# The passages between the sublayers of a hybrid encoder block: one function in a fixed engine order

## The chip, the cores and the metric

The kernel runs on one core of one Trainium2 chip. Its engines work side by side, each through its own queue in order: TensorE (PE) multiplies, VectorE (DVE), ScalarE (ACT) and GpSimd (POOL) work element by element, and SyncE (SP) issues most DMAs. The metric is the device time of one execution in microseconds; for the kernel before it is the median of three runs.

## The reference

One encoder layer over 256 tokens of width 2048, in float32, with three sublayers. A vector c gives, through one large matrix (`w_ada`), a shift, a scale and a gate for each sublayer:

```python
mod = (silu(c) @ w_ada + b_ada)          # 3 x (shift, scale, gate), 2048 each
modulate(h, s) = layer_norm(h) * (1 + scale[s]) + shift[s]

y = swiglu(modulate(x, 0), ffn1_w13, ffn1_w2)                 # d_ff = 5632
x = layer_norm(ALPHA * x + 0.5 * gate[0] * y, ln_g[0], ln_b[0])

proj = modulate(x, 1) @ w_in + b_in      # q, k, v, o, gates, x_rg, g_rg
y = concat(mLSTM(...) , RG-LRU(...)) @ w_out
x = layer_norm(ALPHA * x + gate[1] * y, ln_g[1], ln_b[1])

y = swiglu(modulate(x, 2), ffn2_w13, ffn2_w2)
x = layer_norm(ALPHA * x + 0.5 * gate[2] * y, ln_g[2], ln_b[2])
```

ALPHA is 2 to the power 1/4. Between two sublayers there is thus a chain that nothing can go around: the last products of y, the residual, the statistics of a row, the post-norm with its gain and bias, the statistics again, the second normalisation, a transpose, the modulation, and only then the first products of the next sublayer.

## The kernel before

**Precision.** Every float32 operand of a matmul is split in two float32r parts, high and low, and each product is three matmuls (high x high, high x low, low x high). `load_w` (L80) does that for a weight tile of 128 x 2048: a DMA on SP's queue into one of four raw buffers (L83), a copy to the high part on ACT (L92), a subtraction to the low part on DVE (L95). Three buffers of each kind ("hi", "lo") hold the parts; a fourth pair can come out of the six general slots (`spare`, L64). With `fine` set, both run in four pieces of 512 columns.

**Work.** x stays in SBUF as two row tiles of 128 tokens (t = 0, 1). A sublayer's input u is kept transposed as `uh` and `ul`. `stat_w` (L260) has the weights stationary and moves 256 tokens: 48 matmuls of 128 x 256 per weight tile. `mov_t` (L271) has the activations of one row tile stationary and moves 512 weight columns: 12 matmuls for each weight tile and row tile. `ffn` (L332) goes through groups of hidden columns: g1 makes a group's hidden rows, g2 (L479) multiplies the group before with w2 and adds into yacc (L494). The mixer (L549) runs projections (`proj`, L562), gates, recurrence, heads and the output product.

**adaLN tiles.** The product with w_ada is 144 tiles of 128 x 2048, each a DMA on SP and one DVE instruction with an accumulator (L136). `tick` (L144) hands them out: every weight load adds a rate to a credit, and each whole credit issues one tile. The rates stand in a table (L36 to L39); `ada_until` (L139) forces those that are needed.

**A passage before.** `tail` (L301) makes the last products of a sublayer for row tile 0 and then 1 (tiles named tl), with `residual` (L316) behind each: DVE multiplies with the gate (L320), then DVE or POOL adds to x (L322, L325), and DVE takes statistics (L327). `post_ln` (L236) normalises: DVE three quarters in six instructions (L250, L252), ACT and POOL the last (L245 to L247), then the statistics of the result (L256). `after` (L819) makes the second normalisation n (L190, L191). In the middle of row tile 1 `ahead` loads and splits the first three weight tiles of the next sublayer. `front` (L289) then takes both row tiles in turn: `modulate_t` (L210) makes all sixteen transposes (tu, L216) in four groups, modulates them on ACT and DVE (L221, L223) and splits them (L224, L225); then come the 48 matmuls of that row tile. Credits run on through all of it.

**Order.** The tile framework orders each engine's queue itself, by priorities and a simulated time; the program's text does not fix it.

**Gate columns.** Among the projections `gates` (L611) makes the mLSTM's gates on DVE, in small instructions on 4 x 256, and `gate_cols` (L622) transposes them on PE (pcol, L626 and L627). It stands behind the third pair of x_rg tiles (L687).

Of the kernel before, what the change touches and what calls it, by code (L numbers as in the profile page):

```python
# [15 lines left out]
P = 128  # L16
D = 2048
# [33 lines left out]
def block_kernel(ctx: ExitStack, tc: tile.TileContext, a: dict, out: bass.AP):  # L51
# [28 lines left out]
    def load_w(src, name, into=None):  # L80
        tick()
        raw = raw_tile("r" + name)
        nc.sync.dma_start(raw, src)  # L83
        if into is None:
            hi = wp.tile([P, 2048], F32R, tag="hi", bufs=3, name="h" + name)
            lo = wp.tile([P, 2048], F32R, tag="lo", bufs=3, name="l" + name)
        else:
            hi, lo = into()
        step = 512 if fine[0] else 2048
        for c in range(0, 2048, step):  # L90
            w = slice(c, c + step)
            nc.scalar.copy(hi[:, w], raw[:, w])  # L92
        for c in range(0, 2048, step):
            w = slice(c, c + step)
            nc.vector.tensor_sub(lo[:, w], raw[:, w], hi[:, w].bitcast(F32))  # L95
        return hi, lo

# [87 lines left out]
    def normed(st, t, n, nm, on_vector=0):  # L185

        mv, r, b = moments(st, nm)
        c = on_vector
        if c:
            nc.vector.tensor_scalar(n[:, 0:c], x[:, t, 0:c], mv[:, 0:1], r, op0=ALU.subtract, op1=ALU.mult)  # L190
        nc.scalar.activation(n[:, c:], x[:, t, c:], AF.Identity, bias=b, scale=r)  # L191
# [18 lines left out]
    def modulate_t(s, t, n):  # L210

        tk = slice(t * P, (t + 1) * P)
        for kt in range(0, KT, 4):
            ps = bank(f"tu{s}{t}_{kt}")
            for j in range(4):
                nc.tensor.transpose(ps[:, j * P:(j + 1) * P], n[:, (kt + j) * P:(kt + j + 1) * P], ident)  # L216
            u = sm.tile([P, 4, P], F32, tag="u", bufs=2, name=f"u{s}{t}_{kt}")
            for j in range(4):
                b, g = modc[:, s, 0, kt + j:kt + j + 1], modc[:, s, 1, kt + j:kt + j + 1]
                if j < MOD_ACT[t]:  # L220
                    nc.scalar.activation(u[:, j, :], ps[:, j * P:(j + 1) * P], AF.Identity, bias=b, scale=g)  # L221
                else:
                    nc.vector.tensor_scalar(u[:, j, :], ps[:, j * P:(j + 1) * P], g, b, op0=ALU.mult, op1=ALU.add)  # L223
            nc.scalar.copy(uh[:, kt:kt + 4, tk], u)  # L224
            nc.vector.tensor_sub(ul[:, kt:kt + 4, tk], u, uh[:, kt:kt + 4, tk].bitcast(F32))  # L225

# [8 lines left out]

    def post_ln(s, t, st, gb):  # L236

        nm = f"p{s}{t}"  # L240
        g, b = gb
        mv, r, nb = moments(st, nm)
        out_st = sm.tile([P, 4, 6], F32, tag="st", name="st" + nm)
        c = slice(AFF, D)
        nc.scalar.activation(x[:, t, c], x[:, t, c], AF.Identity, bias=nb, scale=r)  # L245
        nc.gpsimd.tensor_mul(x[:, t, c], x[:, t, c], g[:, c])
        nc.gpsimd.tensor_add(x[:, t, c], x[:, t, c], b[:, c])  # L247
        for k in range(0, AFF, 512):
            c = slice(k, k + 512)
            nc.vector.scalar_tensor_tensor(x[:, t, c], x[:, t, c], mv[:, 0:1], g[:, c],  # L250
                                           op0=ALU.subtract, op1=ALU.mult)
            nc.vector.scalar_tensor_tensor(x[:, t, c], x[:, t, c], r, b[:, c],  # L252
                                           op0=ALU.mult, op1=ALU.add)
        if s < 2:
            for n in range(4):
                nc.vector.bn_stats(out_st[:, n, :], x[:, t, n * 512:(n + 1) * 512])  # L256
        return out_st
# [13 lines left out]
    def mov_t(ps, hl, acth, actl, k0, t, first, last):  # L271

        hi, lo = hl
        tk = slice(t * P, (t + 1) * P)
        for j in range(4):
            w = slice(j * 512, (j + 1) * 512)
            nc.tensor.matmul(ps, acth[:, k0 + j, tk], hi[:, w], start=first and j == 0, stop=False)  # L277
            nc.tensor.matmul(ps, acth[:, k0 + j, tk], lo[:, w], start=False, stop=False)  # L278
            nc.tensor.matmul(ps, actl[:, k0 + j, tk], hi[:, w], start=False, stop=last and j == 3)  # L279
# [5 lines left out]
    def front_tiles(tiles, nm, ks):  # L285
        return [load_w(tiles[k], f"{nm}{k}", spare if k == 3 else None)
                for k in ks]

    def front(s, ns, hls, tiles, nm):  # L289

        hls = hls + front_tiles(tiles, nm, range(len(hls), 4))
        pss = [bank(f"{nm}{t}") for t in range(NT)]
        for t in range(NT):
            modulate_t(s, t, ns[t])
            if t == NT - 1:
                fine[0] = False
            for k in range(4):
                mov_t(pss[t], hls[k], uh, ul, k * 4, t, k == 0, k == 3)
        return pss

    def tail(s, blocks, mm, alpha, sts, gb, ahead):  # L301


        for t in range(NT):
            for i, n in enumerate(blocks):
# [642 lines left out]
```

## Time and profile before

| | |
|---|---|
| median of three runs | 2034.55 us (2031.8 to 2035.66) |
| the profiled execution | 2032.17 us |
| its span, first to last instruction | 2030.4 us |
| mean granted TensorE clock | 0.981 |
| HBM read | 509.22 MB, 252 GB/s over the span |

The profile is of one execution. A row of its timeline has the start in us, the duration in us, the engine, the line, the operation, output <- input, the shapes and the count, and in brackets the idle time before it with what ended it. A row of groups has a bar, then busy time and mean ns of one, and a second bar, then the idle time before them. A row of windows has for each stretch its length, the busy time of PE, PEld, DVE, ACT and POOL with counts, then the granted clock, the share of the DMA engines and GB/s. A row of waits has the waiting instruction, what released it, the sum in us, how often, and the longest. Matmuls are pipelined: a matmul of 128 x 512 is listed with 0.39 us, though the next can start after less.

### The profile page before, as it was taken

To read this page: it belongs to the slowest core of one execution; us is meant where nothing else is said; L and a number is where in the kernel's file an instruction comes from. 1 tells how busy PE (TensorE), PEld (TensorE's weight loads), DVE (VectorE), ACT (ScalarE), POOL (GpSimd) and SP (SyncE) were. 2 spreads that over 40 slices of the span, in tenths; PEclk is the share of its full clock that TensorE was granted. 3 is DMA by queue.
4 is the path that set the end of the run, shared out by engine and by line. 5 is a ranking of instruction groups with operands and counts; after the bars stand their busy time and mean duration, and the time that the engine had idled before them with its cause. 6 is when DMAs were issued, how large, how long until landed. Compare 5 with 4: busy or idle time off the path is not lost.

```text
span 2030.4 us, 30188 instructions
## 1 busy us (share of the span) xinstructions
PE 1926.2 (95%) x13068; PEld 1788.7 (88%) x13068; DVE 1435.2 (71%) x1340; ACT 814.2 (40%) x752; POOL 58.6 (3%) x76
## 2 busy tenths in 40 slices
PE   7899999999999997597999997999999999999996
PEld 6899998799899985497989885899999899899985
DVE  7998898987978889876785778544444544544558
ACT  5433344443334332643743334533443333334332
POOL 0000000000000001200000002000000000000003
PEclk8999999999999999798999998999999999999998
DMA  9998888999998997475677565455555555555552
GB/s 385 340 352 299 306 329 330 359 350 352 367 348 321 351 336 282 160 285 189 241 275 273 208 212 182 166 184 179 184 192 177 194 185 181 195 179 178 193 187 104
DMA packets 72709, 513.27 MB, mean 253 GB/s; under 512 B 8448, under 2 KB 8576, under 8 KB 10880
## 3 DMA queue, kind: packets, MB, share of 16 engines
q1 hardware_dynamic: 69984, 501.25, 67.4%
q10 hardware_dynamic: 2592, 10.09, 1.3%
q8 instruction: 102, 1.67, 0.3%
q14 instruction: 31, 0.25, 0.0%
HBM read 509.22 MB, written 2.10 MB: 252 GB/s over the span
## 4 chain that ended last, share of the span: by engine, by line
PE 87%; DVE 9%; issue 2%; DMA 1%; ACT 1%; POOL 0%; POOLq 0%; SPq 0%; DVEq 0%
PE py L278 6%; PE py L277 6%; PE py L279 6%; PE pg L269 6%; PE pv L268 6%; PE pv L267 6%; PE pv L269 6%; PE pg L268 6%; PE pg L267 6%; PE pj L267 3%; PE pj L269 3%; PE pj L268 3%; DVE ada L136 2%; PE rg L268 2%; PE rg L269 2%
## 5 line engine op out<-in xcount | busy, mean ns | idle before, releaser
L136 DVE CUSTOM_DVE_ANT_0 ada<-ada,scb,badac 128x2048 f32<-128x2048 f32 x144 | 340.0, 2364 | 11.4 <-DMA ada<-in_w_ada 9.6
L269 PE MATMUL pg<-uh,lg 128*128 128x256 f32 x960 | 272.1, 283 | 0.5 <-DVE lg L95 0.5
L269 PE MATMUL pv<-uh,lv 128*128 128x256 f32 x960 | 271.8, 283 | 0.0
L267 PE MATMUL pg<-uh,hg 128*128 128x256 f32 x960 | 271.7, 283 | 0.0
L268 PE MATMUL pv<-ul,hv 128*128 128x256 f32 x960 | 271.7, 283 | 0.0
L267 PE MATMUL pv<-uh,hv 128*128 128x256 f32 x960 | 271.7, 283 | 0.0
L268 PE MATMUL pg<-ul,hg 128*128 128x256 f32 x960 | 271.7, 283 | 0.0
L95 DVE TENSOR_TENSOR lw<-rw,hw 128x2048 fp32r<-128x2048 f32 x80 | 183.3, 2291 | 123.1 <-ACT hw L92 123.1
L278 PE MATMUL py<-lw,hth 128*128 128x512 f32 x640 | 250.3, 391 | 3.7 <-DVE lw L95 3.5
L95 DVE TENSOR_TENSOR lv<-rv,hv 128x2048 fp32r<-128x2048 f32 x68 | 155.8, 2291 | 134.5 <-ACT hv L92 134.5
L279 PE MATMUL py<-hw,htl 128*128 128x512 f32 x640 | 249.1, 389 | 0.0
L92 ACT CAST hw<-rw 128x2048 fp32r<-128x2048 f32 x80 | 152.8, 1911 | 231.0 <-DMA rw<-in_w 73.9
L277 PE MATMUL py<-hw,hth 128*128 128x512 f32 x640 | 242.7, 390 | 0.0
L95 DVE TENSOR_TENSOR lg<-rg,hg 128x2048 fp32r<-128x2048 f32 x60 | 137.5, 2292 | 114.5 <-ACT hg L92 114.5
L92 ACT CAST hv<-rv 128x2048 fp32r<-128x2048 f32 x68 | 129.6, 1906 | 210.9 <-PE pg L268 76.1
L269 PEld LDWEIGHTS pg<-uh,lg 128*128 128x128 f32 x960 | 184.3, 192 | 1.1 <-DVE lg L95 1.1
L92 ACT CAST hg<-rg 128x2048 fp32r<-128x2048 f32 x60 | 114.2, 1904 | 175.4 <-PE pv L268 108.3
L268 PEld LDWEIGHTS pg<-ul,hg 128*128 128x128 f32 x960 | 184.3, 192 | 0.3
L267 PEld LDWEIGHTS pg<-uh,hg 128*128 128x128 f32 x960 | 184.3, 192 | 0.3
L269 PEld LDWEIGHTS pv<-uh,lv 128*128 128x128 f32 x960 | 184.3, 192 | 0.0
L267 PEld LDWEIGHTS pv<-uh,hv 128*128 128x128 f32 x960 | 184.3, 192 | 0.0
L268 PEld LDWEIGHTS pv<-ul,hv 128*128 128x128 f32 x960 | 184.3, 192 | 0.0
(363 smaller groups left out, 4186.8 us busy)
## 6 DMA issues: line engine op xcount, KB each, us to landing
ada<-in_w_ada SPq DMA_DIRECT2D x144, 1024.0 KB, 5.8
rw<-in_w SPq DMA_DIRECT2D x80, 1024.0 KB, 4.8
rg<-in_w SPq DMA_DIRECT2D x60, 1024.0 KB, 4.9
rv<-in_w SPq DMA_DIRECT2D x60, 1024.0 KB, 4.8
rra<-in_w_r SPq DMA_DIRECT2D x48, 1024.0 KB, 5.2
rs<-in_w_s SPq DMA_DIRECT2D x32, 1024.0 KB, 4.8
rwo<-in_w_out SPq DMA_DIRECT2D x16, 1024.0 KB, 4.7
ro<-in_w_vo SPq DMA_DIRECT2D x8, 1024.0 KB, 4.8
```

The source lines that it names most:

```text
L92: nc.scalar.copy(hi[:, w], raw[:, w])
L95: nc.vector.tensor_sub(lo[:, w], raw[:, w], hi[:, w].bitcast(F32))
L136: nc.vector.tensor_tensor_reduce(raw, raw, scb, 1.0, badac[:, s, j, kt:kt + 1], ALU.mult, ALU.add, adac[:, s, j, kt:kt + 1])
L267: nc.tensor.matmul(ps, hi[:, w], uh[:, k0 + j, :], start=st, stop=False)
L268: nc.tensor.matmul(ps, hi[:, w], ul[:, k0 + j, :], start=False, stop=False)
L269: nc.tensor.matmul(ps, lo[:, w], uh[:, k0 + j, :], start=False, stop=sp)
L277: nc.tensor.matmul(ps, acth[:, k0 + j, tk], hi[:, w], start=first and j == 0, stop=False)
L278: nc.tensor.matmul(ps, acth[:, k0 + j, tk], lo[:, w], start=False, stop=False)
L279: nc.tensor.matmul(ps, actl[:, k0 + j, tk], hi[:, w], start=False, stop=last and j == 3)
```

## The change

One function, `boundary`, takes the place of `tail`, `front`, `modulate_t`, `post_ln` and `after`. It issues on DVE, ACT, POOL and TensorE through a wrapper that pins each instruction behind the one traced before it on its engine. The next sublayer's four weight tiles are all loaded at its start; those named in `ready` are split between the residuals of row tile 0, the others between the blocks of row tile 0, one of them with its low part on POOL. Part of the last weights go into uh and ul, whose contents are no longer needed. The credits are zero within a passage. x is scaled by ALPHA beforehand on ACT, so that a residual only adds; the earlier blocks' residuals move to POOL, and those within a passage run on DVE alone. The gate columns move from behind the third to behind the fourth pair of tiles (from 4 to 6).

```diff
-    def load_w(src, name, into=None):
+    def load(src, name, into=None):
         tick()
         raw = raw_tile("r" + name)
         nc.sync.dma_start(raw, src)
+        return raw, name, into
+    def split(tile, act, low):
+        raw, name, into = tile
+        hi, lo = into() if into else [wp.tile([P, 2048], F32R, tag=w, bufs=3, name=w[0] + name) for w in ("hi", "lo")]
         step = 512 if fine[0] else 2048
+        cols = [slice(c, c + step) for c in range(0, 2048, step)]
+        for w in cols:
+            act.copy(cut(hi, w), like(raw[:, w], hi))
+        for w in cols:
+            low.tensor_sub(cut(lo, w), like(raw[:, w], lo), cut(hi, w).bitcast(F32))
         return hi, lo
+    class Pinned:
...
+        def __getattr__(self, op):
+            def issue(*args, **kw):
+                ins = getattr(self.engine, op)(*args, **kw)
+                tc.keep_in_program_order(ins)
+                return ins
+            return issue
+    V, A, G, T = (Pinned(e) for e in (nc.vector, nc.scalar, nc.gpsimd, nc.tensor))
...
+    def half(t):
+        return lambda: [u[:, :, t * P:(t + 1) * P] for u in (uh, ul)]
+    def rows(k):
+        return lambda: [u[:, k:k + 8, :].rearrange("p a b -> p (a b)") for u in (uh, ul)]
-    def residual(s, t, n, y, alpha, sts):
+    def residual(s, t, n, y, sts):
...
-        nc.vector.tensor_mul(g, y, gate[:, c])
-        if alpha:
-            nc.vector.scalar_tensor_tensor(x[:, t, c], x[:, t, c], ALPHA, g, op0=ALU.mult, op1=ALU.add)
-        else:
-            last = t == NT - 1 and (n == 3 or s == 2)
-            (nc.vector if last else nc.gpsimd).tensor_add(x[:, t, c], x[:, t, c], g)
+        (nc.vector if sts else nc.gpsimd).tensor_mul(g, y, gate[:, c])
+        nc.gpsimd.tensor_add(x[:, t, c], x[:, t, c], g)
         if sts:
             nc.vector.bn_stats(sts[t][:, n, :], x[:, t, c])
+    def scale_x():
+        for t in range(NT):
+            nc.scalar.mul(x[:, t, :], x[:, t, :], ALPHA)
...
+    def boundary(s, hls, order, mm, sts, following):
+        g, b = gb = ln_rows(s)
+        ps = {}
+        if following:
+            tiles, nm, ready, in_slots = following
+            fw = [load(tiles[k], f"{nm}{k}", spare if k in in_slots else None) for k in range(4)]
...
+        def take(t, n):
...
+            V.tensor_mul(gy, ps[t, n], gate[:, c])
+            V.tensor_add(x[:, t, c], x[:, t, c], gy)
...
+        def norm(t):
+            mv, r, nb = moments_of(sts[t], f"p{s}{t}")
...
+            A.activation(x[:, t, cs[3]], x[:, t, cs[3]], AF.Identity, bias=nb, scale=r)
+            G.tensor_mul(x[:, t, cs[3]], x[:, t, cs[3]], g[:, cs[3]])
+            G.tensor_add(x[:, t, cs[3]], x[:, t, cs[3]], b[:, cs[3]])
+            for c in cs[:3]:
+                V.scalar_tensor_tensor(x[:, t, c], x[:, t, c], mv[:, 0:1], g[:, c], op0=ALU.subtract, op1=ALU.mult)
+            for n, c in enumerate(cs):
+                if n < 3:
+                    V.scalar_tensor_tensor(x[:, t, c], x[:, t, c], r, b[:, c], op0=ALU.mult, op1=ALU.add)
+                if following:
+                    stats(st, t, n)
+                else:
+                    nc.sync.dma_start(out[t * P:(t + 1) * P, c], x[:, t, c])
+            return st
...
+        def finish_n(t, nn):
+            n, mv, r, nb = nn
+            for k in range(0, D, 512):
+                c = slice(k, k + 512)
+                if k == 0:
+                    V.tensor_scalar(n[:, c], x[:, t, c], mv[:, 0:1], r, op0=ALU.subtract, op1=ALU.mult)
+                else:
+                    A.activation(n[:, c], x[:, t, c], AF.Identity, bias=nb, scale=r)
+            return n
+        def u_of(t, n, k):
...
+            for j in range(4):
+                T.transpose(pt[:, j * P:(j + 1) * P], n[:, (4 * k + j) * P:(4 * k + j + 1) * P], ident)
...
+                if j < 3 or k:
+                    A.activation(u[:, j, :], pt[:, j * P:(j + 1) * P], AF.Identity, bias=h, scale=m)
+                else:
+                    V.tensor_scalar(u[:, j, :], pt[:, j * P:(j + 1) * P], m, h, op0=ALU.mult, op1=ALU.add)
+            A.copy(uh[:, 4 * k:4 * k + 4, tk], u)
+            V.tensor_sub(ul[:, 4 * k:4 * k + 4, tk], u, uh[:, 4 * k:4 * k + 4, tk].bitcast(F32))
+        products(0)
+        for i, n in enumerate(order[0]):
+            for k in ready[i:] if n == order[0][-1] else ready[i:i + 1]:
+                fw[k] = split(fw[k], nc.scalar, nc.vector)
+            take(0, n)
+            stats(sts[0], 0, n)
+        products(1)
+        rest = list(order[1])
...
+        nn = start_n(0, norm(0))
+        late = [k for k in range(4) if k not in ready]
+        if len(rest) > 1:
+            take(1, rest[0])
+        n = finish_n(0, nn)
+        pss.append(bank(f"{nm}0"))
+        for k in range(4):
+            u_of(0, n, k)
+            if k == 0 and len(rest) > 1:
+                stats(sts[1], 1, rest.pop(0))
+            if rest:
+                take(1, rest[0])
+                stats(sts[1], 1, rest.pop(0))
+            if late and k == min(late) - 1:
+                fw[late[0]] = split(fw[late[0]], A, G)
+            elif len(late) > 1 and k == late[1] - 1:
+                fw[late[1]] = split(fw[late[1]], A, V)
+            mov_t(pss[0], fw[k], uh, ul, k * 4, 0, k == 0, k == 3)
+        n = finish_n(1, start_n(1, norm(1)))
+        pss.append(bank(f"{nm}1"))
+        for k in range(4):
+            u_of(1, n, k)
+            mov_t(pss[1], fw[k], uh, ul, k * 4, 1, k == 0, k == 3)
+        fine[0] = False
+        nxt.append(pss)
...
+        credit[:] = 0.0, 0.0
         fine[0] = True
+        hls = [load_w(w2[(NFF // 4 - 1) * 4 + n], f"w2{s}l{n}", (spare, half(0), half(1), None)[n]) for n in range(4)]
+        boundary(s, hls, ((0, 1, 2, 3), (3, 0, 1, 2)), lambda ps, t, n: mov_t(ps, hls[n], hth, htl, 0, t, True, True),
+                 sts, following)
...
-        proj(1, 8, xr, {0: gates, 4: gate_cols})
+        proj(1, 8, xr, {0: gates, 6: gate_cols})
...
+        order = ((2, 3, 0, 1), (2, 0, 3, 1))
+        hls = {k: load_w(a["w_out"][k * 4 + 3], f"wo3{k}", {1: rows(8), 3: spare}.get(k)) for k in order[0]}
...
+        boundary(s, hls, ((3,), (3,)), last, sts, following)
...
+    ffn(0, a["w13_1"], a["w2_1"], start, (a["w_vo"][8:12], "o0", (0, 1, 2), (2,)))
     softplus_lambda()
+    mixer((a["w13_f"], "fg", (0, 1), (1,)))
+    ffn(2, a["w13_2"], a["w2_2"], None)
```

Passage one below is the one from the first FFN to the mixer, passage two the one from the mixer to the second FFN, and the end is what follows the second FFN's last products. A block is one quarter of the next sublayer's first products for one row tile: four transposes, their modulation, and twelve matmuls.

More of the change, by code (lines that the diff above doesn't have):

```diff
@@ L208, in modulate @@
             nc.vector.tensor_sub(ul[:, kt:kt + w, :], u[:, 0:w, :], uh[:, kt:kt + w, :].bitcast(F32))
[L210 to L225, printed above, removed]
     def ln_rows(s):
@@ L283, in mov_w @@
             mov_t(pss[t], hl, acth, actl, k0, t, first, last)
[L285 to L299, printed above, removed]
```

156 lines of the change are left out of this document (75 added, 81 removed).

## The prediction

> **What bounds the kernel now.** I read the page's busy shares first, then the waits of PE, then the timeline and windows around the long ones.
>
> ```profile
> PE 1926.2 (95%) x13068; PEld 1788.7 (88%) x13068; DVE 1435.2 (71%) x1340; ACT 814.2 (40%) x752; POOL 58.6 (3%) x76
> ```
>
> TensorE is busy for 95% of the span and idle for 2030.4 - 1926.2 = 104 us. The change can only shorten the holes in its stream, or make new ones. Two rows of the waits of PE name more than half of them:
>
> ```profile
> PE tu L216 <- ACT n L191: 45.8, 2, 32.6
> PE pcol L626 <- DVE gg L617: 10.5, 1, 10.5
> ```
>
> The 45.8 us are the two passages between sublayers, the 10.5 us the gate columns. The timeline of PE gives the passages' edges:
>
> ```profile
> 729.26 0.63 PE L277 MATMUL py<-hw,hth 128*128 128x512 f32 x2
> 776.53 0.39 PE L279 MATMUL py<-hw,htl 128*128 128x512 f32 x1
> 835.02 3.62 PE L216 MATMUL tu<-ident,n 128*128 128x128 f32 x16 [32.60 <-ACT n L191]
> 863.28 0.62 PE L277 MATMUL po<-ho,uh 128*128 128x512 f32 x2
> ...
> 1223.61 0.39 PE L277 MATMUL tl<-hwo,rh 128*128 128x512 f32 x1
> 1245.14 0.39 PE L279 MATMUL tl<-sh,ul 128*128 128x512 f32 x1
> 1258.78 3.37 PE L216 MATMUL tu<-ident,n 128*128 128x128 f32 x16 [13.25 <-ACT n L191]
> 1263.07 0.50 PE L277 MATMUL fg<-hfg,uh 128*128 128x512 f32 x1 [0.91 <-ACT uh L224]
> 1287.35 0.62 PE L277 MATMUL fv<-hfv,uh 128*128 128x512 f32 x2
> ```
>
> Passage two: 96 tail matmuls from 1223.61 to 1245.14, which is 0.227 us each; a hole; 96 more with 32 transposes until 1287.35. I count a passage from its first tail matmul (T0) to the next sublayer's first matmul after it: 1287.35 - 1223.61 = **63.7 us** in passage two. In passage one py ends near T0 = 776.8, and 863.28 - 776.8 = **86.5 us**. Behind the one hole PE never waits long again: in this order all transposes and both row tiles' LayerNorms come early. The windows show who works in the holes:
>
> ```profile
> 730.00:777.00 47.00, 44.72 (x193) 35.43 (x192) 45.48 (x45) 16.48 (x15) 0.00 (x0) 1.00 0.91 335
> 803.00:836.00 33.00, 0.98 (x5) 0.99 (x6) 32.52 (x47) 9.29 (x18) 13.13 (x12) 0.57 0.57 202
> 936.00:941.00 5.00, 4.95 (x23) 4.93 (x24) 2.01 (x5) 0.00 (x0) 0.00 (x0) 0.51 0.34 141
> 941.00:946.00 5.00, 5.00 (x43) 4.85 (x42) 0.17 (x1) 1.49 (x2) 0.00 (x0) 1.00 0.00 0
> ```
>
> In the first hole (803 to 836) DVE is busy for 32.52 of 33 us. Before it DVE is full too (45.48 of 47). After a hole of 10 us PE issues 23 matmuls in 5 us at clock 0.51 and then 43: a restart costs about 2 us more.
>
> **The change, part by part.**
>
> *adaLN tiles.* Counting the credits through the loads, seven tiles (four beside the last w2 tiles, three beside the next weights) leave passage one. Each is one DVE instruction and one 1 MB DMA on SP:
>
> ```profile
> L136 DVE CUSTOM_DVE_ANT_0 ada<-ada,scb,badac 128x2048 f32<-128x2048 f32 x144 | 340.0, 2364 | 11.4 <-DMA ada<-in_w_ada 9.6
> ```
>
> That is 7 x 2.36 = 16.5 us of DVE in the stretch that is bound by DVE. By the same count six of them end beside the second FFN's first groups, where no adaLN tile stands now: there one adds 2.36 us of DVE to 2.29 for a weight tile, beside 48 x 0.12 = 5.6 us of PE. No cost.
>
> *New order inside a passage.* What follows is my chain for one passage, from these rows of passage two:
>
> ```profile
> 1235.82 0.69 DVE L320 TENSOR_TENSOR gy<-tl,gate 128x512 f32<-128x512 f32 x1 [7.51 <-PE tl L279]
> 1237.28 0.69 DVE L327 BATCH_NORM_STATS2 sts<-x 128x6 f32<-128x512 f32 x1
> ...
> 1255.06 0.25 DVE L174 BATCH_NORM_AGGREGATE mvn<-stp 128x2 f32<-128x24 f32 x1
> 1255.90 0.27 DVE L174 BATCH_NORM_AGGREGATE mvp<-sts 128x2 f32<-128x24 f32 x1
> 1256.31 0.29 ACT L182 ACTIVATE nbn<-nbn,rsn 128x1 f32<-128x1 f32 x1 [0.76 <-POOL rsn L163]
> 1256.63 2.10 ACT L191 ACTIVATE n<-x,nbn,rsn 128x2048 f32<-128x2048 f32 x1
> 1262.77 0.69 DVE L256 BATCH_NORM_STATS2 stp<-x 128x6 f32<-128x512 f32 x1
> 1275.58 1.03 PE L216 MATMUL tu<-ident,n 128*128 128x128 f32 x8
> 1276.22 1.51 ACT L221 ACTIVATE u<-tu,adac 128x128 f32<-128x128 f32 x4 [2.46 <-PE tu L216]
> 1277.88 1.32 ACT L224 CAST uh<-u 128x512 fp32r<-128x512 f32 x2 [0.15 <-DVE u L223]
> 1278.53 1.39 DVE L225 TENSOR_TENSOR ul<-u,uh 128x512 fp32r<-128x512 f32 x2
> ```
>
> Row tile 0's products take 10.9 us. Its last residual chain is 1237.28 + 0.69 - 1235.82 = 2.15 us, so its statistics are there at T0 + 13.3. In passage one DVE must also split three weight tiles (2.4 us each) between the residuals: 3 x 2.4 + 4 x 1.8 = 14.4, so T0 + 14.3. LayerNorm to its last statistics takes 1263.46 - 1255.90 = 7.6 us.
>
> Then the blocks. The transposes of block k + 1 are pinned behind what was traced before them on PE, and that is the twelve matmuls of block k. So a block is serial: 0.64 us from the first transpose to ACT (1275.58 to 1276.22), four ACT instructions 1.51, copy 0.62, two handovers 0.1: 2.87 us until its first matmul; the third matmul needs ul, 0.69 behind the copy, and loses 0.33; then 12 x 0.227 = 2.72. Sum **5.92 us**, of which PE works 0.52 + 2.72 = 3.24. Before, the transposes were issued eight or sixteen together, ahead of the matmuls, and ACT ran beside PE.
>
> The first block starts behind the norm: 1256.31 + 0.29 - 1255.06 = 1.54 us to the bias, about 1.9 us for three ACT quarters of n (estimate from 2.10 us for all four in one), three u instructions 1.16, copy 0.67: 5.27 us to the first matmul, 8.3 to the end of the block. Row tile 0 is done at 8.3 + 3 x 5.92 = 26.1 us.
>
> Row tile 1's norm stands on DVE behind the last subtraction of row tile 0, at 8.3 + 2 x 5.92 + 2.87 + 0.74 = 23.75 us. Queued behind it: its own n, ACT's u, all PE work. So PE stands still from 26.1 to 23.75 + 7.6 + 5.27 = 36.6: a new hole of 10 us. From row tile 0's statistics the passage lasts 7.6 + 23.75 + 7.6 + 26.1 = 65.0, with two restarts of 2 us 69.0 us.
>
> Passage two: 13.3 + 69.0 = 82.3 against 63.7: **+18.6 us**. (Bounds: +13 with 0.6 us less in each norm and no slow restart; +24 with 1.5 us more in each norm and a block longer by 0.4.) Passage one: 14.3 + 69.0 = 83.3 against 86.5: **-3.2 us**, if T0 stays.
>
> *Weights split ahead.* The instructions stay as many; they move. On SP the four loads of the next weights come without adaLN loads between them, ln_g and ln_b stay on ACT's queue, and with four raw buffers tiles 2 and 3 wait for the subtractions of tiles 0 and 1:
>
> ```profile
> ro<-in_w_vo SPq DMA_DIRECT2D x8, 1024.0 KB, 4.8
> ```
>
> A load that is issued at T0 has landed at T0 + 4.8 and is split 2.5 us later: inside the 10.9 us of products, so nothing. Without that cover each late microsecond is one of the passage, since row tile 0's residual is pinned behind the subtraction. The tiles split late (ACT 2.2 us, POOL 4 x 1.28 = 5.1) lie beside the 5.9 us of a block: nothing. Weights that lie in uh and ul are read in runs of 128 columns; no row shows that. Between nothing and, at half rate, 48 x 0.227 = 10.9 us in either FFN's tail; I take nothing, as the transposed u is written and read in such runs.
>
> *Residual on POOL.* This moves T0 of passage one. Sixteen DVE instructions leave the last g2 before it, sixteen POOL instructions come. The nearest rows:
>
> ```profile
> 762.38 0.70 DVE L322 SCALAR_TENSOR_TENSOR x<-x,gy 128x512 f32<-128x512 f32 x1
> 762.98 0.69 DVE L494 TENSOR_TENSOR yacc<-yacc,py 128x512 f32<-128x512 f32 x1
> ...
> 792.58 2.48 DVE L95 TENSOR_TENSOR lw20l<-rw20l,hw20l 128x512 fp32r<-128x512 f32 x4
> 802.37 4.16 POOL L325 TENSOR_TENSOR x<-x,gy 128x512 f32<-128x512 f32 x3 [3.49 <-ACT ho L92]
> 803.94 3.73 DVE L95 TENSOR_TENSOR lo<-ro,ho 128x512 fp32r<-128x512 f32 x3
> 836.07 1.28 POOL L246 TENSOR_TENSOR x<-x,ln_g 128x512 f32<-128x512 f32 x1 [2.92 <-ACT x L245]
> ```
>
> DVE starts its next instruction 0.60 us after such a residual (762.38 to 762.98), so 16 x 0.6 = 9.6 us go. Four subtractions alone take 2.48 us; three beside three POOL instructions take 3.73 instead of 1.86, so each POOL instruction costs DVE 0.62 us. Then 16 x 0.62 = 9.9 us come: T0 stays. Bounds: nothing conflicts and the stretch is bound by PE (eight tiles of 24 x 0.227 = 43.6 instead of 47.3, -3.7 us); every POOL instruction shuts DVE out for its full 1.28 (20.5 for 9.6: +10.9). [...]
>
> The other residuals and the x scaling on ACT (4 us per sublayer, ACT at 40%) lie beside PE work: nothing. If DVE had no slack in the second FFN's last g2, its POOL instructions would cost up to 2 us.
>
> *Gate columns.* They move two weight tiles later, 96 matmuls at 43 in 5 us: 11.2 us. The hole of 10.5 us and a restart of 2.2 go. New: one more weight subtraction stands in DVE's row ahead of the last gate instruction,
>
> ```profile
> 936.05 0.26 PE L626 MATMUL pcol<-ident,gg 4*128 4x4 f32 x1 [10.54 <-DVE gg L617]
> 927.37 2.29 DVE L95 TENSOR_TENSOR ls<-rs,hs 128x2048 fp32r<-128x2048 f32 x1 [1.12 <-ACT hs L92]
> 937.64 0.40 DVE L620 TENSOR_TENSOR gg<-gg 4x256 f32<-4x256 f32 x1
> ```
>
> which ends at 938.04 + 2.3 = 940.3, and PE arrives at 925.5 + 11.2 = 936.7: up to 3.6 us, about 1.2 taken. **-11.5 us** (-12.7 to -9).
>
> *The end.* No weights follow, and DVE alone adds the residuals. Row tile 1's last product comes at T0 + 21.8; DVE, behind row tile 0's norm, is through with four residuals about 1 us earlier than now, and the rest stays:
> ```profile
> 2020.95 0.26 DVE L174 BATCH_NORM_AGGREGATE mvp<-sts 128x2 f32<-128x24 f32 x1
> 2025.85 1.59 POOL L247 TENSOR_TENSOR x<-x,ln_b 128x512 f32<-128x512 f32 x1
> ```
>
> 6.5 us from the aggregate to POOL's last addition, 3 us until the span ends. **-1 us** (-2.6 to +1).
>
> Sum: 18.6 - 3.2 - 11.5 - 1 = **+2.9 us**. The profiled execution took 2032.17 us (span 2030.4), so 2035.1; the median of the three runs is 2.4 us above it, so **2038 us** on the scale of the runs.
>
> **The rivals.**
>
> *DVE and POOL shut each other out:* every POOL instruction costs DVE its 1.28 us. Passage one +10.9, and each of the four norms, where POOL's two instructions meet DVE's six, about 0.6 more: +13 in all, **2051**. [...] For it: the 3.73 us. Against: POOL can run beside DVE's PSUM readers and beside bn_stats, as at 836.07.
>
> *Faster, by ACT running ahead.* If a block's u were ready when PE ends the block before, each of six blocks per passage would lose 2.68 us less. It decides where the transposes stand: as soon as they are issued before the matmuls of the block before, ACT needs 2.13 us per block against PE's 3.24. That gives 6 x 2.68 = 16 us per passage: **2006**. Against: the pin as written.
>
> *Faster, by short waits.* Same order, but POOL hardly collides (-3.7), the norms take 0.6 us less (-2.4 over both passages), no restart is slow (-8), the gates fit (-1.2), the end gains all (-1.6): **2021**.
>
> *Nothing happens:* the instruction order comes out as before, **2034.5**.
>
> **How the numbers follow.** A measurement of this kernel can tell about 0.2%, 4 us, from no change. Forecast 0.45 (slower 0.30, same 0.11, faster 0.04), shutting out 0.20 (slower), ACT ahead 0.10 (faster), short waits 0.20 (faster 0.19, same 0.01), nothing 0.05 (same). So faster 0.33, same 0.17, slower 0.50. The forecast's own range is 2029 to 2047. Down to the short waits with some room below and up past the shutting out with passage two's bound gives 2014 to 2056; ACT ahead stays out.
>
> **What would show it.** Right: PE waits for uh about 2.4 us before each block of twelve matmuls, sixteen times over both passages; two holes instead of one per passage, the second about 10 us; pcol's wait under 3.5 us; no ada rows within the passages. Wrong: eight transposes or more in one PE row in the passages, row tile 1's norm on DVE before row tile 0's last subtraction, or T0 of passage one moved by over 6 us.

## The result: slower by 2.4%, and the profile after

The changed kernel takes 2083.09 us (median of four runs, 2079.97 to 2086.13) against 2033.17 us for the kernel before on the same chip: ratio **1.0244**, 95% interval 1.0223 to 1.0265. The sign of the forecast holds; +50 us is far above the +2.9 that the sum gave. The waits of PE in the changed kernel (us in total, times, longest); its pinned instructions all show the wrapper's line, L118:

```profile
PE tu L118 <- DVE n L118: 34.0, 4, 18.6
PE o L267 <- ACT uh L118: 23.8, 7, 5.9
PE fg L267 <- ACT uh L118: 21.5, 7, 4.7
PE tl L267 <- ACT sh L94: 3.8, 2, 2.5
```

Four waits for n where there were two, fourteen for uh where the kernel before had two short ones (0.9 and 0.3 us), and no row for pcol. The timeline of PE gives the edges:

```profile
778.98 0.50 PE L267 MATMUL tl<-sh,hth 128*128 128x512 f32 x1 [1.28 <-ACT sh L94]
819.68 0.69 PE L118 MATMUL tu<-ident,n 128*128 128x128 f32 x2 [18.64 <-DVE n L118]
824.84 0.80 PE L267 MATMUL o<-ho,uh 128*128 128x512 f32 x1 [4.05 <-ACT uh L118]
832.01 0.50 PE L267 MATMUL o<-ho,uh 128*128 128x512 f32 x1 [2.25 <-ACT uh L118]
849.42 0.39 PE L269 MATMUL o<-ho,ul 128*128 128x512 f32 x1
856.27 1.11 PE L118 MATMUL tu<-ident,n 128*128 128x128 f32 x4 [6.46 <-DVE n L118]
886.50 0.48 PE L267 MATMUL po<-ho,uh 128*128 128x512 f32 x1
...
1237.49 0.39 PE L267 MATMUL tl<-hwo,rh 128*128 128x512 f32 x1
1260.90 0.66 PE L118 MATMUL tu<-ident,n 128*128 128x128 f32 x4 [1.49 <-DVE n L118]
1266.24 0.80 PE L267 MATMUL fg<-hfg,uh 128*128 128x512 f32 x1 [4.69 <-ACT uh L118]
1299.96 1.12 PE L118 MATMUL tu<-ident,n 128*128 128x128 f32 x4 [7.37 <-DVE n L118]
1305.31 0.80 PE L267 MATMUL fg<-hfg,uh 128*128 128x512 f32 x1 [4.23 <-ACT uh L118]
1327.37 0.47 PE L267 MATMUL fv<-hfv,uh 128*128 128x512 f32 x1
...
2038.12 0.50 PE L267 MATMUL tl<-sh,hth 128*128 128x512 f32 x1 [2.48 <-ACT sh L94]
```

From these edges and those of before (where the last T0 is 1992.63; the span goes from 2030.4 to 2078.2), with passages counted as in the prediction:

| stage | before | after | forecast | measured |
|---|---|---|---|---|
| start to T0 of passage one | 776.8 | 779.0 | 0 | +2.2 |
| passage one | 86.5 | 107.5 | -3.2 | **+21.0** |
| the mixer, with the gate columns | 360.3 | 351.0 | -11.5 | -9.3 |
| passage two | 63.7 | 89.9 | +18.6 | **+26.2** |
| the second FFN to T0 of the end | 705.3 | 710.8 | 0 | +5.5 |
| the end | 37.8 | 40.1 | -1 | +2.3 |

The sum missed by 44.9 us, and 31.8 of them lie in the two passages. The edges even hide some: in the changed kernel PE fills the wait of a passage's last block with the first products behind the passage, and makes that block's twelve matmuls (2.7 us) later. So 2.7 us of the passage stand in the mixer's row, and as many in that of the second FFN. Windows over the twelve matmuls of single blocks of the changed kernel (length, then busy time of PE, PEld, DVE, ACT and POOL, then the granted clock):

```profile
824.84:829.20 4.36, 4.36 (x13) 3.37 (x14) 3.26 (x5) 0.00 (x0) 0.00 (x0) 0.64 0.00 0
832.01:835.20 3.19, 3.19 (x13) 2.28 (x14) 2.67 (x4) 0.00 (x0) 0.00 (x0) 1.00 0.01 3
1266.24:1271.50 5.26, 5.26 (x12) 3.98 (x13) 2.66 (x4) 0.00 (x0) 0.00 (x0) 0.50 0.00 0
```

The block at 832 has the full clock and takes 3.3 us to the modelled end of its last matmul. One other of the 14 blocks that stand alone does; the twelve that are left have a clock of 0.50 to 0.65 and take 4.4 to 5.5 us. The mean of all is 4.7 where the forecast had 3.05. And the timeline of DVE, ACT, SP and POOL, most of it ahead of passage one:

```profile
757.54 2.77 DVE L96 TENSOR_TENSOR lw<-rw,hw 128x2048 fp32r<-128x2048 f32 x1
758.12 3.34 POOL L287 TENSOR_TENSOR gy<-yacc,gate 128x512 f32<-128x512 f32 x1
760.24 3.38 DVE L163 CUSTOM_DVE_ANT_0 ada<-ada,scb,badac 128x2048 f32<-128x2048 f32 x1
770.14 5.79 DVE L96 TENSOR_TENSOR ul<-rw20l,uh 128x512 fp32r<-128x512 f32 x4
781.65 4.68 DVE L96 TENSOR_TENSOR sl<-rw20l,sh 128x512 fp32r<-128x512 f32 x4
786.25 2.49 DVE L96 TENSOR_TENSOR lw20l<-rw20l,hw20l 128x512 fp32r<-128x512 f32 x4
786.35 19.27 SPq L84 DMA_DIRECT2D ro<-in_w_vo  x5
793.48 2.50 DVE L96 TENSOR_TENSOR lo<-ro,ho 128x512 fp32r<-128x512 f32 x4 [4.75 <-ACT ho L94]
809.41 0.26 DVE L118 BATCH_NORM_AGGREGATE mvp<-sts 128x2 f32<-128x24 f32 x1
...
2037.45 2.19 ACT L94 CAST sh<-rw22l 128x512 fp32r<-128x512 f32 x4 [7.46 <-POOL gy L287]
2037.49 1.28 POOL L288 TENSOR_TENSOR x<-x,gy 128x512 f32<-128x512 f32 x1
```

Beside POOL's residuals four subtractions take 4.7 to 5.8 us and not 2.49, and an adaLN tile 3.38 and not 2.36; a POOL instruction takes 3.34, and 1.28 at 2037.49, where it starts ahead of DVE's next instruction (2038.10). The raw buffers come free late: the subtraction that starts at 781.65 ends at 786.33, and the next weights are first asked for at 786.35, T0 + 7.4. Row tile 0's statistics, held behind their subtractions, come at T0 + 30.4, not T0 + 14.3.

### The profile page after: what moved, and what is told of

It is laid out like the page before. It is cut to its first block, busy times and chain, and to the rows that moved or that the text cites. A ratio compares the mean times of both kernels' runs of the same rounds, so it can differ in the third digit from the quotient of the medians.

```text
span 2078.2 us, 30197 instructions
## 1 busy us (share of the span) xinstructions
PE 1949.3 (94%) x13068; PEld 1800.0 (87%) x13068; DVE 1434.1 (69%) x1287; ACT 837.4 (40%) x788; POOL 132.7 (6%) x111
## 5 line engine op out<-in xcount | busy, mean ns | idle before, releaser
L163 DVE CUSTOM_DVE_ANT_0 ada<-ada,scb,badac 128x2048 f32<-128x2048 f32 x144 | 341.8, 2376 | 20.4 <-DMA ada<-in_w_ada 18.3
```

Source lines behind the costliest of these rows:

```text
L163: nc.vector.tensor_tensor_reduce(raw, raw, scb, 1.0, badac[:, s, j, kt:kt + 1], ALU.mult, ALU.add, adac[:, s, j, kt:kt + 1])
```

## The experiments

Theory: four costs lie in the passages. (1) Serial blocks, by the held transposes, and the low clock that they bring. (2) POOL's residuals, which delay the raw buffers and so the next weights. (3) The scaling of x, which stands in the passage on ACT. (4) The held order on the other engines. The rivals stand with each run. Times are medians; before lay at 2032.3 to 2034.0 us in these sessions.

**Transposes one block ahead** (on the changed kernel)

```diff
+        turn(0, n, 0)
         for k in range(4):
+            if k < 3:
+                turn(0, n, k + 1)
             u_of(0, n, k)
```

`turn` holds the four transposes that `u_of` made before; row tile 1 has the same.

> The changed kernel with the four transposes of block k+1 issued (and pinned) ahead of the matmuls of block k; nothing else. Theory 'serial blocks': six of the eight blocks of a passage lose their wait of 2.25 us, and TensorE, no longer interrupted every 7 us, gets its clock back, so that twelve matmuls take about 3 us and not 4.5 to 5.5. A block goes from 7.3-8.5 to about 4, minus some 2 us by which the second hole grows since row tile 1's norm stays behind row tile 0's last subtraction: -18 us per passage, about 2047 us, ratio to before 1.007. Rival 'the clock is low because of the long hole, not because of the short waits': only the waits go, -13 us per passage, about 2057 (1.012). Rival 'the pins are not what binds': same as the changed kernel, 2083 (1.024).

Measured: 2046.85 us, 1.0063 [1.0047, 1.0079], -36 us: the first theory's number. Its waits of PE:

```profile
PE tu L118 <- DVE n L118: 35.3, 4, 18.0
PE o L267 <- ACT uh L118: 8.7, 3, 5.1
PE fg L267 <- ACT uh L118: 7.9, 3, 4.1
```

And windows over two blocks that come behind the first of their row tile:

```profile
833.60:836.60 3.00, 3.00 (x17) 2.43 (x15) 0.66 (x2) 2.71 (x7) 0.00 (x0) 1.00 0.03 12
1284.80:1287.80 3.00, 3.00 (x16) 2.45 (x15) 1.25 (x1) 3.00 (x5) 0.00 (x0) 1.00 0.00 0
```

The waits for uh fall from 45.3 to 16.6 us, which is 28.7 of the 36; the holes stay as long as they were. In these two blocks behind the first the clock is now 1.00, and sixteen and seventeen PE instructions lie in 3.00 us, so there the short waits held it down and not the long holes.

**The earlier residuals back on DVE**

```diff
-        (nc.vector if sts else nc.gpsimd).tensor_mul(g, y, gate[:, c])
-        nc.gpsimd.tensor_add(x[:, t, c], x[:, t, c], g)
+        nc.vector.tensor_mul(g, y, gate[:, c])
+        nc.vector.tensor_add(x[:, t, c], x[:, t, c], g)
```

> The changed kernel with both residual instructions of the sublayers' earlier tiles back on DVE (mul and add there; x stays scaled by ACT). Theory 'GpSimd's residuals collide with DVE, so the subtractions end late, the raw buffers come free late and the next weights are loaded late': in passage one the next weights' first load is issued some 8 us earlier against T0, the first hole of TensorE shrinks from 18.6 to 9-11 us, T0 moves by less than 3 us; 2074 us, ratio 1.020. Rival 'the weights are late because the split buffers or the queue are': first hole unchanged, T0 later by up to 2 us, 2083-2087 (1.024-1.026).

Measured: 2071.59 us, 1.0186 [1.0171, 1.0202], -11.5 us. From its timeline:

```profile
781.50 17.53 SPq L84 DMA_DIRECT2D ro<-in_w_vo  x5
802.80 0.26 DVE L118 BATCH_NORM_AGGREGATE mvp<-sts 128x2 f32<-128x24 f32 x1
813.08 0.48 PE L118 MATMUL tu<-ident,n 128*128 128x128 f32 x1 [12.49 <-DVE n L118]
```

The weights are asked for 4.9 us earlier, the statistics come 6.6 us earlier and the hole is 6.1 us shorter: theory (2), by less than the 8 us expected. T0 is 778.5. The two profiled executions differ by 8.4 us: 5.8 lie in passage one, 2.7 in the second FFN, where the stage falls from 710.8 to 708.1. The rest of the hole remains: the load is issued at T0 + 3 and lands 4.8 us later, and the residuals still stand behind it.

**Splits taken from between the residuals** (on the kernel with DVE's residuals)

```diff
-            for k in ready[i:] if n == order[0][-1] else ready[i:i + 1]:
-                fw[k] = split(fw[k], nc.scalar, nc.vector)
...
         for k in range(4):
+            if k in ready:
+                fw[k] = split(fw[k], nc.scalar, V)
             u_of(0, n, k)
```

> The kernel with the earlier residuals on DVE, and in it the splits of the next weights taken from between row tile 0's residuals and put one ahead of each block, so that the residuals wait for no load. Theory 'row tile 0's residuals stand behind the subtractions of weights that land late': in passage one row tile 0's statistics come about 10 us earlier, the first hole goes from 12.5 to about 4 us; in passage two one subtraction now stands ahead of the first block, +2.5: in all -6 us, 2065 (1.0155). Rival 'DVE has the same sum of work before the first block either way': 2070-2074 (1.0185).

Measured: 2067.63 us, 1.0170 [1.0145, 1.0194]. The interval overlaps that of the kernel that it starts from, so the time decides nothing. The waits do: PE's longest wait for n is 7.3 us, not 12.5, and in passage two the first wait for uh is 6.6, not 4.7. So residuals that were held behind a load were 5 us of the first hole. In passage two a subtraction now stands ahead of the first block.

**The scaling of x.** Two edits. The first asks that the mixer's scaling be issued behind an og instruction:

```diff
+        with tc.issue_after(last_og[0].ins):
-        scale_x()
+            scale_x()
```

> The changed kernel with the mixer's two scalings of x issued behind the output gate's first additions, so that they can't stand inside passage one. Theory 'an instruction that is not pinned slips between two pinned ones on ACT': the first block of each row tile waits 1.9 us less for uh (4.05 and 5.93 us in the changed kernel): -4 us, 2079 (1.022). Rival 'ACT would have waited there anyway': 2083 (1.024).

Measured: 2083.83 us, 1.0255 [1.0237, 1.0274]. It tells nothing, since the timeline of ACT shows the scaling still between u and the copy to uh:

```profile
821.41 1.13 ACT L118 ACTIVATE u<-tu,adac 128x128 f32<-128x128 f32 x3
822.44 1.90 ACT L294 ACTIVATE x<-x 128x2048 f32<-128x2048 f32 x1
824.24 0.61 ACT L118 CAST uh<-u 128x512 fp32r<-128x512 f32 x1
```

The second holds the scalings in program order, behind the passage:

```diff
-            nc.scalar.mul(x[:, t, :], x[:, t, :], ALPHA)
+            A.mul(x[:, t, :], x[:, t, :], ALPHA)
```

> The changed kernel with the scalings of x held in program order too, so that on ACT they stand behind all of the passage (in the earlier edit they did not move). Theory 'the scaling, 1.9 us, delays the copy of the first block by about 1.5 us in each of the four row tiles': -6 us, 2077 (1.0215); the first wait for uh goes from 4.05 and 4.7 us to 2.6 and 3.2. Rival 'something else makes the copy late': 2083 (1.0245).

Measured: 2073.57 us, 1.0198 [1.0183, 1.0213], -9.5 us. The first waits for uh go from 4.05 and 4.69 to 2.83 and 3.47 us: theory (3). An instruction that was not held had slipped between two held ones. The four first waits are shorter by 1.2 us each, 4.9 in all. The two profiled executions differ by 6.6 us, and all of it lies in passage two (83.2 us, it was 89.9): in passage one (107.3, it was 107.5) other blocks than before are slow, and together with a second wait for n of 7.60 us for 6.46 they take the shorter waits back: from its first matmul to its twelfth the first block takes 4.86 us for 4.10, the second 4.34 for 2.91, and the fourth 2.94 for 4.09. So the scaling cost between 5 and 9.5 us, and how much of the rest is the clock's doing stays open.

**Nothing held**, and **transposes alone not held**

```diff
-    V, A, G, T = (Pinned(e) for e in (nc.vector, nc.scalar, nc.gpsimd, nc.tensor))
+    V, A, G, T = nc.vector, nc.scalar, nc.gpsimd, nc.tensor
...
+    V, A, G, T = *(Pinned(e) for e in (nc.vector, nc.scalar, nc.gpsimd)), nc.tensor
```

> The changed kernel with no instruction held in program order: same functions, same instructions, the scheduler places them. Theory 'the held order of the transposes costs, not the function's order': transposes of blocks 1 to 3 come ahead of the first block's matmuls, the waits of 2.25 us go, about -15 us per passage, 2053 us (1.010). Rival 'the function's order itself costs (norm of row tile 1 late, weights late)': within 6 us of the changed kernel, 2077-2089.

> The changed kernel with the transposes alone not held in program order; the instructions of DVE, ACT and GpSimd stay held. Theory 'two costs: transposes held (serial blocks), and row tile 1's norm held on DVE behind row tile 0's last subtraction': like the kernel with the transposes issued one block ahead, 2047 us (1.006), two holes in each passage, the second 7 to 9 us. Rival 'the transposes are all of it': like the kernel with nothing held, 2027 us (0.996), one hole per passage.

Measured: nothing held 2026.71 us, 0.9964 [0.9953, 0.9976], a little faster than before and far below both times that were expected; transposes not held 2041.49 us, 1.0033 [1.0018, 1.0047], between the two that were expected (2047 and 2027). The wait for n among the waits of PE, with the transposes not held:

```profile
PE tu L380 <- DVE n L118: 36.1, 4, 18.8
```

And with nothing held:

```profile
PE tu L380 <- DVE n L370: 34.8, 2, 26.7
```

The held transposes cost 42 us. The other 15 lie in the held order of DVE, ACT and GpSimd. With nothing held DVE does both norms ahead of the blocks: the hole before them grows (26.7), but a passage has one. PE waits for n as long in all (34.8 us for 36.1) and less for uh (12.3 for 19.2), and the passages are 6.5 and 7.5 us shorter.

**Which engine's order holds the second norm back?** Four runs on the kernel with the transposes not held: row tile 1's norm placed earlier, in the loop over row tile 0's blocks; DVE's order free too; ACT's order free too; and both, so that GpSimd's alone is held.

```diff
+            if not rest and st1 is None:
+                st1 = norm(1)
...
-        n = finish_n(1, start_n(1, norm(1)))
+        n = finish_n(1, start_n(1, st1))
...
+    V, A, G, T = nc.vector, Pinned(nc.scalar), Pinned(nc.gpsimd), nc.tensor
...
+    V, A, G, T = Pinned(nc.vector), nc.scalar, Pinned(nc.gpsimd), nc.tensor
...
+    V, A, G, T = nc.vector, nc.scalar, Pinned(nc.gpsimd), nc.tensor
```

> The kernel with only the transposes not held, and in it row tile 1's LayerNorm issued on DVE as soon as its last residual is there (in passage two behind row tile 0's first block, in passage one behind the third) and not behind row tile 0's last subtraction. Theory 'the place of that norm in the held order of DVE makes the second hole': the second hole, 8.4 and 7.4 us, shrinks by 6 to 8 us in each passage, the subtraction behind the norm comes up to 4 us late: -6 to -12 us on 2041, about 2032 (0.999). Rival 'DVE's work is a fixed sum, the hole only moves': 2039-2044 (1.003).

> The changed kernel with transposes and DVE's instructions not held; ACT's and GpSimd's stay held. With the transposes alone not held it took 2041.5 us, with nothing held 2026.7: 15 us lie in the held order of DVE, ACT or GpSimd. Theory 'it is DVE's: between row tile 0's first statistics and row tile 1's n it idles some 12 us of 39 for ACT, with row tile 1's norm at hand but held behind': 2029 us (0.998), second hole under 3 us. Rival 'it is ACT's held order': 2040 (1.003).

> The changed kernel with transposes and ACT's instructions not held; DVE's and GpSimd's stay held. Theory 'it is DVE's held order': no more than 3 us better than with the transposes alone not held, 2039-2042 us (1.003), second hole of 6 us or more in each passage. Rival 'it is ACT's held order': 2029 (0.998).

> The changed kernel with GpSimd's instructions alone held; those of TensorE, DVE and ACT not. Theory 'GpSimd's held order makes the second hole by itself: row tile 1's reciprocal root stands there behind the subtraction of a late weight tile, 5.5 us that wait for the tile's copy on ACT, so DVE and ACT can't go on with that norm whatever their own order': like the kernels in which DVE or ACT was set free as well as the transposes, 2036-2040 us (1.002-1.0035), the second hole over 4 us. Rival 'it takes the held orders of several engines': 2030 us or less (0.998), near the kernel with nothing held.

Measured: norm earlier 2040.24 us, 1.0041 [1.0026, 1.0056]; DVE free 2040.36, 1.0035 [1.0022, 1.0047]; ACT free 2036.36, 1.0016 [1.0006, 1.0025]; GpSimd alone held 2021.01, 0.9940 [0.9923, 0.9956]. The earlier norm, and DVE set free, were expected to give 9 to 12 us and gave 1; the theory that GpSimd's held order makes the second hole by itself failed as well (2036 to 2040 us expected). With the earlier norm the second wait for n is gone,

```profile
PE tu L380 <- DVE n L118: 19.7, 2, 18.2
```

but waits of up to 6.5 us for uh and 3.7 us for ul come in its place. Neither engine's order is it alone: free together, DVE and ACT give 20 us, one by one 1 and 5. The timeline of the kernel with DVE free, in passage two:

```profile
1248.29 0.26 DVE L300 BATCH_NORM_AGGREGATE mvp<-sts 128x2 f32<-128x24 f32 x1
1255.86 2.18 ACT L118 CAST hfg<-rfg 128x512 fp32r<-128x512 f32 x4
1256.56 5.51 POOL L118 TENSOR_TENSOR lfg<-rfg,hfg 128x512 fp32r<-128x512 f32 x4 [10.94 <-ACT hfg L118]
1262.03 0.66 POOL L118 TENSOR_SCALAR vep<-mvp 128x1 f32<-128x1 f32 x1
1264.34 3.10 DVE L352 SCALAR_TENSOR_TENSOR x<-x,rsp,ln_b 128x512 f32<-128x512 f32 x3
```

DVE, free, had the statistics at 1248.6, but the root of the variance stood on POOL behind the subtraction of a late weight tile, that subtraction waited for the tile's copy, and the copy was held on ACT behind row tile 0's u. So the norm went on at 1264.3. In the kernel with GpSimd alone held POOL has the same order; its timeline at the same place:

```profile
1228.28 2.17 ACT L94 CAST hfg<-rfg 128x512 fp32r<-128x512 f32 x4
1234.07 6.09 POOL L118 TENSOR_TENSOR lfg<-rfg,hfg 128x512 fp32r<-128x512 f32 x4
1239.80 0.26 DVE L300 BATCH_NORM_AGGREGATE mvp<-sts 128x2 f32<-128x24 f32 x1
1240.15 0.78 POOL L118 TENSOR_SCALAR vep<-mvp 128x1 f32<-128x1 f32 x1
```

ACT, free, made the copy in the first hole; the late subtraction was done by 1240.16, and the root's first instruction came 0.1 us behind the end of the statistics, not 13.5. The held order is a chain over three queues: an engine set free stops at the next one.

**The parts outside the passages, on the kernel before**: `gate_cols` at 6 instead of 4; the credits at zero in the passages, as in the changed kernel; both.

```diff
-        proj(1, 8, xr, {0: gates, 4: gate_cols})
+        proj(1, 8, xr, {0: gates, 6: gate_cols})
...
             pg = front(s, ns, nxt.pop(), a["w13_f"], "fg")
+            credit[:] = -2.0, FFN2_RATE
...
         hth, htl = hts[len(groups) - 1]
+        credit[:] = 0.0, 0.0
         fine[0] = True
...
```

The mixer has the same two lines, with its own rate, and the old starting credits of both go.

> The kernel before with the gate columns made two weight tiles later; nothing else. Theory 'hole and restart go': -11.5 us as in the prediction, up to -12.7, 2022 us (0.994), and no wait of pcol. Rival 'the wait moves to another instruction behind the same chain of DVE': 2034 (1.000).

> The kernel before without adaLN tiles in and just before the two passages (the credits set as in the changed kernel); nothing else. Theory 'DVE, 32.5 of 33 us busy, sets the first hole of passage one': seven instructions of 2.36 us leave, -7 (three of them, those in the hole) to -16 us (all seven), about 2024 (0.995). Rival 'another chain (loads, ACT) is late next': within 3 us, 2031-2034 (0.999-1.000).

> The kernel before with two parts of the change alone: the gate columns two weight tiles later and no adaLN tiles in the passages; the passages themselves as before. Theory 'the two gains are in different stages and add': -16.8 and -10.5 us, about 2006 us (0.987), faster than both kernels. Rival 'the adaLN tiles that now come later fill the stretch in which the gates are made': 2012 or more (0.990).

Measured: 2022.66 us, 0.9949 [0.9932, 0.9966]; 2017.08, 0.9922 [0.9905, 0.9939]; both **2007.70, 0.9869** [0.9849, 0.9889]. The gate columns and the sum came as expected; the credits gave 16.8 us, just above the upper end of what was expected (7 to 16). The two add (0.9949 x 0.9922 = 0.9871). The wait for n among the waits of PE with both:

```profile
PE tu L216 <- ACT n L191: 33.7, 2, 20.4
```

No pcol, and the first hole is 20.4 us instead of 32.6. That is 12.2 us of the seven tiles' 16.5 (7 x 2.36), so not all of them were on its path. With the credits alone the hole is 20.3 us and the wait of pcol falls by 2.4 us as well, from 10.5 to 8.1.

**Repairs of the changed passages.** Transposes not held, norm earlier and residuals on DVE; nothing held and residuals on DVE; the same with the scaling held behind the copies to uh.

```diff
-            nc.scalar.mul(x[:, t, :], x[:, t, :], ALPHA)
+            Pinned(nc.scalar).mul(x[:, t, :], x[:, t, :], ALPHA)
...
-            A.copy(uh[:, 4 * k:4 * k + 4, tk], u)
+            Pinned(A).copy(uh[:, 4 * k:4 * k + 4, tk], u)
```

The last of the three has this edit; the others join edits shown above.

> The kernel with only the transposes not held, with both repairs: row tile 1's LayerNorm as soon as its residuals are there, and the earlier residuals on DVE. Theory 'the places of single steps cost, not the holding': the gains add, 2041.5 - 9.5 - 12 = 2020 us (0.993), near the kernel with nothing held and the residuals on DVE, 2013.7. Rival 'a held order costs as such, since the chip's times differ from the plan': 2028 or more (0.997).

> Nothing held in program order, and the residuals of the earlier tiles on DVE. Theory 'GpSimd's residuals delay the split weights and so the first hole, whatever the order': -12 us on the kernel with nothing held, 2015 (0.991), first hole of passage one from 26.7 to about 18 us. Rival 'with nothing held, the weights fit in anyway': 2027 (0.996), hole unchanged.

> Nothing held but the copies to uh and, behind them, the scalings of x, and the earlier residuals on DVE. Theory 'the scaling delays the first copies of a passage, here too': -4 us on 2013.7, about 2009 us (0.988), level with the kernel before with the two parts alone (2007.7). Rival 'with nothing held ACT has room for it': 2012-2015 (0.990).

Measured: 2029.77 us, 0.9981 [0.9971, 0.9990]; 2013.65, 0.9903 [0.9887, 0.9919]; 2012.92, 0.9903 [0.9888, 0.9918]. The first had been expected at 2020, as if the gains added: the earlier norm gives next to nothing while the engines' order is held. POOL's residuals cost 10.5 to 13 us in all three orders tried. With nothing held the place of the scaling makes no difference that these runs can tell (4 us were expected). Repaired, the new passages beat the kernel before, but the old passages with the two other parts, 2007.70, are at least level with them.

## Why the prediction was wrong, step by step

The signs that the prediction names for itself came: waits for uh ahead of the blocks, two holes per passage, no wait of pcol over 3.5 us, T0 moved by 2.2 us. The time did not, above all since two steps failed: the price of a block's matmuls, and the cover that was counted on for the next weights.

- **Serial block**: the mechanism is right (2.25 us of wait in seven of the blocks, 3.5 to 5.9 in the others; the working has 2.87 from the first transpose). The term that was mis-sized is its matmuls: 3.05 us forecast, 4.7 measured, since the clock is 0.50 to 0.65 in twelve of the 14 blocks; counted the same way, a block at full clock takes 3.3. "Two restarts of 2 us" per passage put that price at the two long holes only. Fourteen blocks times 1.35 are 19 us, for which 8 were allowed.
- **Weights split ahead**: "inside the 10.9 us of products, so nothing" failed. Its own next sentence came true: "each late microsecond is one of the passage". The load was issued at T0 + 7.4, since the raw buffers were late, and the statistics came 16 us late in passage one. That is the largest part of the 24.2 us by which the forecast missed this passage. (The forecast's 14.3 is 14.4 by its own terms.) The runs give 6.6 us of the 16 to POOL's residuals and some 5 to residuals held behind a load; no run tells the rest apart.
- **Residual on POOL**: "T0 stays" holds within 2.2 us, and it was the wrong place to look. The collisions delay buffers: 11.5 us in all. The prediction's upper bound of +10.9, with DVE shut out for the full 1.28 us of each POOL instruction, is near the 11.5 as a sum, though only some 6 of the 11.5 us lie in passage one. In the rows the two sides end as if by turns: POOL's instruction of 758.12 ends 1.15 us behind DVE's subtraction of 757.54, and 1.28 is what one took at 2037.49, ahead of DVE's next instruction; DVE's adaLN tile of 760.24 ends 2.16 us behind that, and 2.36 is its mean. So both sides come out longer (3.34 us for 1.28, 3.38 for 2.36), and the 0.62 us that the prediction took for each POOL instruction rested on one row of three subtractions.
- **x scaling "beside PE work: nothing"** failed: 5 to 9.5 us.
- **Second hole of 10 us**: 13.5 us (849.8 to 863.3) and 12.7 (1292.6 to 1305.3) from row tile 0's last matmul to row tile 1's first, for a forecast of 10.5. With the scaling behind the passage the wait for uh in each is 1.2 us shorter; the holes are then 13.4 and 10.2. The forecast named DVE's queue; the runs show that ACT's and POOL's queues hold that norm as well.
- **adaLN tiles**: -16.5 us of DVE for passage one; alone the credits gave -16.8, of which 12.3 are the first hole and 2.4 the gate columns' wait, so the closeness is in part luck. No cost came where the tiles went: the second FFN's stage has 705.3 us with and without them.
- **Gate columns**: -11.5 forecast, -11.2 alone. In the changed kernel the stage gives -9.3, and -12.0 without the 2.7 us of the passage's last block that stand in it.
- **The second FFN and the end**: 0 and -1 forecast, +5.5 and +2.3 measured. Of the 5.5, 2.7 are the last block of passage two. At the stage's end PE waits 2.48 us for a weight tile's copy into a slot that POOL's residual held until then; with the residuals on DVE that wait falls to 0.5 us and the stage by 2.7. The prediction had "up to 2 us" for it, under a condition, and left it out of its sum. Why the end itself is longer was not tried; it takes 37.8 us, as before, with nothing held and the residuals on DVE, and 40.4 or 40.5 with one of the two alone.
- **The rivals**: "ACT running ahead" priced transposes ahead at 16 us a passage; the run gave 18, of which 14 are waits for uh; the clock, which the price left out, came on top, so that the two figures lie this close is luck in part. In the changed kernel itself it was not at work. "Shutting out" had 13 us against 10.5 to 13, at other places, so its nearness is luck in part; its mechanism was there beside the forecast's own, not in its stead.

Open: why GpSimd's held order alone is 6 us better than nothing held.

## What to carry to other kernels

An order fixed by hand couples the queues: before it is fixed, ask for each held instruction what stands behind it on its engine, and whether a load, a late split or an instruction that isn't held can get ahead of it. A wait of 2.25 us every 6.0 to 8.2 us cost twice here, once as the wait and once as the clock: in five of the seven blocks with it twelve matmuls took 4.5 to 4.9 us, and 3.3 in the two at the full clock. Run the parts of a large change one by one: here two small ones gave 1.3%, and the whole with the new passages lost 2.4%.

## What the runs showed of the hardware

Waits of 2.25 us between bursts of twelve matmuls went with a low granted clock: 0.61 to 0.63 in five of the seven blocks with just this wait, 0.50 to 0.65 behind each longer one, and 1.00 without it in the two blocks shown of the kernel that makes its transposes one block ahead. The seven blocks start 6.0 to 8.2 us behind the block before.

A value like 0.61, that of the block at 838 in the changed kernel (838.00 to 842.40), is a mean. Windows over the wait ahead of this block and over parts of the block:

```profile
835.40:838.00 2.60, 0.36 (x4) 0.12 (x2) 0.02 (x1) 2.17 (x6) 0.00 (x0) 1.00 0.00 0
838.00:838.20 0.20, 0.20 (x1) 0.20 (x2) 0.20 (x1) 0.20 (x1) 0.00 (x0) 1.00 0.00 0
838.30:841.60 3.30, 3.30 (x9) 2.29 (x8) 2.75 (x4) 1.73 (x4) 3.05 (x3) 0.50 0.35 79
841.70:842.40 0.70, 0.70 (x4) 0.57 (x4) 0.00 (x0) 0.00 (x0) 0.70 (x1) 1.00 0.46 178
```

The clock is 1.00 throughout the wait, 0.50 in the middle of the block and 1.00 at its end. Why two of the seven blocks kept the full clock was not shown.
